# One decoder layer in fp32r passes: gate blocks as two column pairs, parked sums placed elsewhere, gelu as one ScalarE operation

## The chip, the cores and the metric

The kernel runs on one core of one Trainium2 chip. Its engines each work through their own instructions in order: TensorE (PE, matmuls), VectorE (DVE), ScalarE (ACT), GpSimd (POOL) and SyncE (SP), and the last two mostly issue DMAs. The metric is the device time of one execution in microseconds. Before the change it is 1453.33 us, the median of 3 runs (1453.3 to 1454.87).

## What is computed

One layer of a decoder trunk on 256 tokens of width 2048, all in float32: a norm, one combined projection, two attention branches (multi-head latent attention A, and banded sliding-window attention B), each passed through its output projection and multiplied by a sigmoid gate, their sum projected, and then a gated feed-forward network with a short causal convolution.

```python
  h  = RMSNorm_pre(x)
  P  = h @ W_in   # q-latent | kv-latent | rope key | SWA q, k, v | branch gates (2 x D_MODEL)
  y  = W_out( sigmoid(gA) * (A @ Wo_A) + sigmoid(gB) * (B @ Wo_B) )
  x  = x + RMSNorm_post(y)
  x  = x + RMSNorm_post2( ConvFFN( RMSNorm_pre2(x) ) )

def conv_ffn(h, w_up, conv_w, conv_b, w_down):
    a, b = jnp.split(h @ w_up, 2, axis=-1)
    ap = jnp.pad(a, ((0, 0), (CONV_WIDTH - 1, 0), (0, 0)))
    c = conv_b
    for j in range(CONV_WIDTH):
        c = c + conv_w[j] * ap[:, j:j + S]
    return (jax.nn.gelu(c, approximate=True) * b) @ w_down
```

The feed-forward width is 5632, so that the layer's weights, read once, are most of the 324 MB that it reads.

## The kernel before

**Matmuls and weights.** Every matrix product is made from three passes: both operands are split into a high part (rounded to the fp32r type) and a low part, and `mm3` (L197) adds high times high, high times low and low times high. The feed-forward up part does the same in another arrangement (`gemm_cols`, L1340 and L1344). Weights come in chunks of 512 KB on SyncE's queue into a ring of raw tiles; `convert` (L152) makes `whi` with an ACT copy (L163) and `wlo` with a DVE subtraction (L164), into a ring of converted pairs. PE uses them some chunks later, so DVE runs ahead of PE by as much as the ring holds (`RING = 4`, and two more where the flexible tiles are given to it).

**Order.** The program is written as a sequence of ticks: after each chunk of a matrix product `tick()` emits what `at(t, ...)` has booked for that tick. The instructions of each engine then stand in one fixed order, and an instruction that waits holds up all behind it on its engine.

**Seven products for eight.** `pair_gemm` (L273) computes two neighbouring column blocks of 512 together, over all 16 row blocks of the weights, in units of two row blocks. A plain unit "p" needs 24 matmuls of 512 columns (two row blocks, two token tiles, two column blocks, three passes). A unit "s" forms seven products of sums, as fast matrix multiplication does, 21 matmuls, but needs sums of token tiles (`token_sums`, here `x_sums`) and of weights: four DVE subtractions of 128x512 (`weight_sums`), and closing sums at the end. A string such as `GATE_ORDER` gives the sequence of units.

**Parked sums.** For the down products the weight sums are made ahead: `park_sums` (L237) loads two row blocks of 512 KB on POOL's queue into a staging tile, makes four subtractions in place on DVE (L252, in the order of the program: `even`, and a tick later `odd`), and stores the results to DRAM on POOL's queue (L257, L262), from where the down products load them as weights. `load` is booked 5 ticks ahead of `even`. Most units share one staging tile (`STAGE`, tag "sg"), so that a unit's load has to wait for the stores of the one before. The names in the trace are `ta_s` (the staging tile of the units for the first down products, twelve units), `ta` (the stored sums), and `tb_s`, `tc_s`, `tw_s` for others of the kind. Before the change, four of the twelve are made in the gate stage (`EARLY = 4`, with two tiles of their own), and eight in the first up part, 7.5 ticks apart (L1375).

**Gates.** Four column blocks of 512 make the B gate. `gate_b` computes one block alone, `gate_pair` two as a pair; `out_b` computes the output projection of the same columns and multiplies. Before the change the order is block 0 alone, `out_b(0)`, blocks 1 and 2 as a pair with three units "s", `out_b(1)`, block 3 alone, `out_b(2)`; `out_b(3)` stands in the latent attention. Ahead of them runs the product for the kv latent, whose result ACT reads out (L726, L727).

**First up part.** `ffn_up0` and then `ffn_up` for column blocks 1 to 5 compute the two halves `ua` and `ub` of the up projection. A block takes 16 ticks, 8 chunks for each half. The results are read out into `f` (L1361 on ACT, L1362 on DVE), and `conv_cols` (L1227) makes the convolution (`cc`, L1232 to L1234), the tanh form of gelu (`uu`, L1235 to L1238: Square, an operation of DVE, Tanh, an operation of DVE) and the product with the other half (L1239), 44 times in the run. In `ffn_up0` its input comes through transposes (`fT`).

Of the kernel before, what the change touches and what calls it, by code (L numbers as in the profile page):

```python
# [11 lines left out]
F32 = mybir.dt.float32  # L12
F32R = mybir.dt.float32r
# [6 lines left out]
P = 128  # L20
# [18 lines left out]
GELU_C = math.sqrt(2.0 / math.pi)  # L39
GELU_R = math.sqrt(0.044715)  # L40


def trunk_layer(ctx, tc, x, x_cols_in, conv_cols_in, g_mix_post, g_ffn_post, w_in, w_q, w_kv,
# [717 lines left out]
    at(now[0] + 4, lambda tr=tr: tr(1))  # L761
    acc, _ = gemm(XH, XL, w_in, 0, KT, C_KV, KVR + ROPE)
# [25 lines left out]
    def gate_b(j):  # L788
        acc, _ = gemm(XH, XL, w_in, 0, KT, C_GB + 512 * j, 512)
        tb = []  # L790
        for t in range(NT):
            g = stg(f"tb{j}_{t}")
            act.activation(g, acc[t], AF.Tanh, scale=rh[:, t:t + 1])
            tb.append(g)
        return tb

    def out_b(j, tb, ps=None):
        acc, _ = gemm(OH, OL, wo_b, 0, KT, 512 * j, 512, ps=ps)
        for t in range(NT):
            vec.scalar_tensor_tensor(tb[t], tb[t], 1.0, acc[t], op0=ALU.add, op1=ALU.mult)  # L800
            pool.dma_start(yb_d[j, t], tb[t])

    STAGE = dict(pl=base, tag="sg")
    es1.close()
    esb.close()
    esg, pg = open_pool("pg")
    xs = {}

    def x_sums(u):
        st = sb(pg, [P, 1024], f"xs{u}", F32R)  # L810
        a, m = (sb(pg, [P, 512], f"x{n}{u}", tag="x" + n, bufs=1) for n in "am")
        xs[u] = token_sums(xt[u].bitcast(F32), a, m, st[:, 0:512], st[:, 512:1024])
# [5 lines left out]
    def gate_pair(j):  # L818
        d = [stg(f"tb{j + i}_{t}") for t in range(NT) for i in range(2)]
        c = pair_gemm("g", w_in, 0, C_GB + 512 * j, GATE_ORDER, lambda k, t: (XH(k)[:, t * P:(t + 1) * P], XL(k)[:, t * P:(t + 1) * P]),  # L820
                      lambda u: xs[u], 0, d, g_place, lambda: [sb(pg, [P, 1024], f"gt{n}{cnt[0]}", tag="gt" + n, bufs=2) for n in "ab"])
# [6 lines left out]
        return [d[0], d[2]], [d[1], d[3]]  # L828

    tb = {0: gate_b(0)}  # L830
    for u in range(GATE_ORDER.count("s")):
        at(now[0] + 3 * u, lambda u=u: x_sums(u))
    out_b(0, tb[0], (pss, "s"))
    tb[1], tb[2] = gate_pair(1)
    parked_b2 = []
    parked_a = [park_a(i, pg, "gr", now[0] + 5 + 5 * i, bufs=2) for i in range(EARLY)]
    out_b(1, tb[1], (pss, "s"))
    tb[3] = gate_b(3)
    out_b(2, tb[2])
# [156 lines left out]
    out_b(3, tb[3])  # L996
# [163 lines left out]
    def x2_norm(t):  # L1160
# [66 lines left out]
    def conv_cols(k, a, b, slot):  # L1227
# [7 lines left out]
        act.activation(uu, cc, AF.Square, scale=GELU_R)  # L1235
        vec.scalar_tensor_tensor(uu, uu, 1.0, cc, op0=ALU.add, op1=ALU.mult)
        act.activation(uu, uu, AF.Tanh, scale=GELU_C)
        vec.scalar_tensor_tensor(uu, uu, 1.0, cc, op0=ALU.add, op1=ALU.mult)  # L1238
# [3 lines left out]
    def norm_row():  # L1242
# [3 lines left out]
        for t in range(NT):  # L1246
            vec.tensor_scalar(dg[:, t * P:(t + 1) * P], ident, rf[t][0][:, 0:1], None, op0=ALU.mult)
# [15 lines left out]
    def ffn_up0():  # L1263
# [88 lines left out]
    def ffn_up(c, slot0):  # L1352
# [288 lines left out]
```

## Time and profile before

| | |
|---|---|
| median of 3 runs | 1453.33 us (1453.3 to 1454.87) |
| the profiled execution, its own time | 1454.23 us |
| its span in the trace | 1452.5 us |
| granted TensorE clock, mean | 0.998 |
| matmuls in the trace | 7518 |
| busy share of DMA queue q1 (SyncE and the like), of q0 (POOL) | 59.8%, 15.0% |
| read from and written to memory | 323.6 MB, 34.7 MB |

The trace is of one execution; its own time is 1.7 us over its span (what lies around the program's instructions), and 0.9 us over the median. In the rows below, a line such as L164 is the kernel's line, then come engine, operation and tile names (result, arrow, operands, with buffer numbers left out), the shape in partitions x elements, the count, and behind a bar the busy time and the mean duration of one; the last part is the idle time ahead of these instructions and what ended it. An instruction's shown duration includes some overlap with the next on the same engine, so the distance from start to start is the better price where many follow each other.

### The profile page before, as it was taken

The page shows a single profiled execution, that of the slowest core. Times are in us where ns is not written, and L with a number is a line of the kernel's source. Part 1 is how long each engine was busy: PE and PEld are TensorE (multiplying, and loading weights), DVE is VectorE, ACT ScalarE, POOL GpSimd, SP SyncE. Part 2 cuts the span into 40 slices and gives each one's busy share as a digit, 9 for nine tenths or more (in the row PEclk, how much of TensorE's full clock was granted, in tenths as well). Part 3 has the DMA queues.
Part 4 walks back from the last instruction along what each step waited for, and adds up shares of the span by engine and source line. Part 5 has one row for each costly group of instructions (what it writes and reads, how often), then busy time and mean ns, then how long its engine had stood idle before and what let it go on. Part 6 is the DMA issues. An engine that isn't in the chain of part 4 may idle for free.

```text
span 1452.5 us, 21438 instructions
## 1 busy us (share of the span) xinstructions
PE 1442.0 (99%) x7518; PEld 1233.7 (85%) x7518; DVE 1160.4 (80%) x2056; ACT 864.7 (60%) x1422; POOL 118.2 (8%) x222
## 2 busy tenths in 40 slices
PE   9999999999999999999999999999999999999997
PEld 7888888888898888888888888888888888888886
DVE  7788896766878775888789899876777797987798
ACT  7588864544555655546566565655646565555673
POOL 2022110010000001100000111000000101000000
PEclk9999999999999999999999999999999999999999
DMA  8655376699875759965666898866878888789965
GB/s 309 209 171 163 103 261 188 219 327 294 244 220 178 230 164 319 348 232 183 219 205 208 272 331 288 292 206 210 310 276 262 312 276 292 246 265 309 340 219 203
DMA packets 164684, 359.69 MB, mean 248 GB/s; under 512 B 20816, under 2 KB 31952, under 8 KB 164576
## 3 DMA queue, kind: packets, MB, share of 16 engines
q1 hardware_dynamic: 143152, 282.49, 59.8%
q0 software_dynamic: 21280, 75.56, 15.0%
q8 instruction: 59, 0.97, 0.3%
q14 instruction: 49, 0.40, 0.1%
q10 hardware_dynamic: 144, 0.26, 0.1%
HBM read 323.62 MB, written 34.65 MB: 247 GB/s over the span
## 4 chain that ended last, share of the span: by engine, by line
PE 91%; DVE 4%; ACT 2%; DMA 2%; issue 1%; SPq 0%; DVEq 0%; ACTq 0%
PE ub L1340 10%; PE ua L1340 9%; PE accg L200 9%; PE accg L198 9%; PE accg L199 9%; PE ub L1344 5%; PE ua L1344 5%; PE cd L199 2%; PE cd L198 2%; PE cd L200 2%; DVE wlo L164 2%; DMA raw<-in_ffn_w_up_dram 1%; PE cdc L199 1%; PE cdc L198 1%; PE cdc L200 1%
## 5 line engine op out<-in xcount | busy, mean ns | idle before, releaser
L163 ACT CAST whi<-raw 128x1024 fp32r<-128x1024 f32 (+2 forms) x497 | 504.0, 1023 | 373.9 <-PE accg L200 109.1
L164 DVE TENSOR_TENSOR wlo<-raw,whi 128x1024 fp32r<-128x1024 f32 (+2 forms) x497 | 585.0, 1188 | 172.0 <-ACT whi L163 165.6
L198 PE MATMUL accg<-whi,ahl 128*128 128x512 f32 (+1 forms) x416 | 162.5, 391 | 0.0
L200 PE MATMUL accg<-whi,ahl 128*128 128x512 f32 (+1 forms) x416 | 160.7, 386 | 0.0
L199 PE MATMUL accg<-wlo,ahl 128*128 128x512 f32 (+1 forms) x416 | 159.8, 384 | 0.0
L1340 PE MATMUL ub<-ahl,whi 128*128 128x512 f32 x640 | 154.7, 391 | 0.2 <-DVE uu L1239 0.2
L1340 PE MATMUL ua<-ahl,whi 128*128 128x512 f32 x640 | 154.6, 391 | 0.0
L1340 PEld LDWEIGHTS ub<-ahl,whi 128*128 128x128 f32 x640 | 117.5, 188 | 23.1 <-ACT cc L1232 0.5
L1340 PEld LDWEIGHTS ua<-ahl,whi 128*128 128x128 f32 x640 | 117.6, 188 | 22.7
L198 PE MATMUL accg<-whi,bhl 128*128 128x512 f32 x256 | 100.8, 394 | 0.0
L200 PE MATMUL accg<-whi,bhl 128*128 128x512 f32 x256 | 100.0, 391 | 0.0
L199 PE MATMUL accg<-wlo,bhl 128*128 128x512 f32 x256 | 99.9, 390 | 0.0
L200 PEld LDWEIGHTS accg<-whi,ahl 128*128 128x128 f32 x416 | 78.1, 188 | 15.2
L199 PEld LDWEIGHTS accg<-wlo,ahl 128*128 128x128 f32 x416 | 78.3, 188 | 13.0
L198 PEld LDWEIGHTS accg<-whi,ahl 128*128 128x128 f32 x416 | 78.2, 188 | 12.9
L1344 PEld LDWEIGHTS ub<-ahl,wlo 128*128 128x128 f32 x640 | 82.2, 191 | 3.3
L1344 PEld LDWEIGHTS ua<-ahl,wlo 128*128 128x128 f32 x640 | 82.2, 191 | 3.1
L1344 PE MATMUL ua<-ahl,wlo 128*128 128x256 f32 x640 | 83.7, 283 | 0.0
L1344 PE MATMUL ub<-ahl,wlo 128*128 128x256 f32 x640 | 83.3, 283 | 0.0
L200 PEld LDWEIGHTS accg<-whi,bhl 128*128 128x128 f32 x256 | 48.1, 188 | 10.1
L199 PEld LDWEIGHTS accg<-wlo,bhl 128*128 128x128 f32 x256 | 48.1, 188 | 9.6
L198 PEld LDWEIGHTS accg<-whi,bhl 128*128 128x128 f32 x256 | 48.1, 188 | 9.6
(659 smaller groups left out, 2679.7 us busy)
## 6 DMA issues: line engine op xcount, KB each, us to landing
raw<-in_ffn_w_up_dram SPq DMA_DIRECT2D x142, 512.0 KB, 4.9
raw<-in_w_in_dram SPq DMA_DIRECT2D x105, 512.0 KB, 4.6
raw<-in_ffn_w_down_dram SPq DMA_DIRECT2D x66, 512.0 KB, 5.6
xraw<-in_ffn_w_up_dram SPq DMA_DIRECT2D x34, 512.0 KB, 5.2
raw<-in_w_o_swa_dram SPq DMA_DIRECT2D x32, 512.0 KB, 5.3
raw<-in_w_o_mla_dram SPq DMA_DIRECT2D x26, 512.0 KB, 6.9
raw<-in_w_out_dram SPq DMA_DIRECT2D x26, 512.0 KB, 4.6
ta_s<-in_ffn_w_down_dram POOLq DMA_DIRECT2D x24, 512.0 KB, 5.9
```

The source lines that it names most:

```text
L163: act.copy(hi[:, a:b], raw[:, a:b])
L164: vec.tensor_tensor(lo[:, a:b], raw[:, a:b], hi[:, a:b].bitcast(F32), op=ALU.subtract)
L198: pe.matmul(o, ah, bh, start=start, stop=False)
L199: pe.matmul(o, ah, bl, start=False, stop=False)
L200: pe.matmul(o, al, bh, start=False, stop=stop)
L1340: pe.matmul(acc[i], hi[:, c], hn[p][:, j * 512:(j + 1) * 512], start=p + j == 0, stop=stop)
L1344: pe.matmul(acc[i][:, 0:256], lo[:, c], hn[p][:, j * 512:j * 512 + 256], start=False, stop=False)
```

## The change

Three things are changed.

The four gate blocks become two pairs, (0, 1) and (2, 3), each with three units "s". The sums of the token tiles are made earlier, in the product for the kv latent, and the pool that they lie in is opened there. `out_b` takes its gate tiles through a function, since the pair's tiles are made when its closing sums are.

Of the twelve parked units for the first down products, none is made in the gates any more. Two are made in the latent attention (`EARLY = 2`), through the common staging tile, behind the `tw` and `tc0` units, which stand 6 ticks apart in place of 7. The other ten stand in the first up part, 6 ticks apart in place of 7.5, starting at the fifth tick in place of the eighth.

Gelu is one ACT operation in place of Square, Tanh and two DVE operations. The factor 0.5 that the tanh form needed goes out of the read-out of `f`, whose operations become a plain copy and a plain addition. The size of a filler tile (`LINE_Z`) becomes 64 in place of 48.

```diff
--- before.py
+++ after.py
@@ -36,8 +36,6 @@
 C_GA = 3392
 C_GB = 5440
-GELU_C = math.sqrt(2.0 / math.pi)
-GELU_R = math.sqrt(0.044715)
 
 
 def trunk_layer(ctx, tc, x, x_cols_in, conv_cols_in, g_mix_post, g_ffn_post, w_in, w_q, w_kv,
@@ -759,6 +757,24 @@
     nrm()
     at(now[0] + 3, lambda tr=tr: tr(0))
     at(now[0] + 4, lambda tr=tr: tr(1))
+    STAGE = dict(pl=base, tag="sg")
+    xs = {}
+
+    def x_sums(u):
+        st = sb(pg, [P, 1024], f"xs{u}", F32R)
+        a, m = (sb(pg, [P, 512], f"x{n}{u}", tag="x" + n, bufs=1) for n in "am")
+        xs[u] = token_sums(xt[u].bitcast(F32), a, m, st[:, 0:512], st[:, 512:1024])
+
+    def to_gates():
+        nonlocal esg, pg
+        es1.close()
+        esb.close()
+        esg, pg = open_pool("pg")
+
+    esg = pg = None
+    at(now[0] + 4, to_gates)
+    for u in range(GATE_ORDER[0].count("s")):
+        at(now[0] + (5, 7, 11)[u], lambda u=u: x_sums(u))
     acc, _ = gemm(XH, XL, w_in, 0, KT, C_KV, KVR + ROPE)
     krd = []
     for t in range(NT):
@@ -785,58 +801,40 @@
     yb_d = dram.tile([4, NT, P, 512], F32, name="yb_d")
     x2_d = dram.tile([NT, P, D], F32, name="x2_d")
 
-    def gate_b(j):
...
-        return tb
-
-    def out_b(j, tb, ps=None):
+    def out_b(j, tb_of, ps=None):
         acc, _ = gemm(OH, OL, wo_b, 0, KT, 512 * j, 512, ps=ps)
+        tb = tb_of()
         for t in range(NT):
             vec.scalar_tensor_tensor(tb[t], tb[t], 1.0, acc[t], op0=ALU.add, op1=ALU.mult)
             pool.dma_start(yb_d[j, t], tb[t])
 
-    STAGE = dict(pl=base, tag="sg")
-    es1.close()
-    esb.close()
-    esg, pg = open_pool("pg")
...
     def g_place():
         both = sb(pg, [P, D], f"gr{cnt[0]}", tag="gr", bufs=2)
         return both[:, 0:1024], both[:, 1024:2048]
 
-    def gate_pair(j):
-        d = [stg(f"tb{j + i}_{t}") for t in range(NT) for i in range(2)]
-        c = pair_gemm("g", w_in, 0, C_GB + 512 * j, GATE_ORDER, lambda k, t: (XH(k)[:, t * P:(t + 1) * P], XL(k)[:, t * P:(t + 1) * P]),
-                      lambda u: xs[u], 0, d, g_place, lambda: [sb(pg, [P, 1024], f"gt{n}{cnt[0]}", tag="gt" + n, bufs=2) for n in "ab"])
+    def gate_pair(j, order):
+        d = []
+
+        def gate_tiles():
+            d[:] = [stg(f"tb{j + i}_{t}") for t in range(NT) for i in range(2)]
+            return d
+
+        c = pair_gemm(f"g{j}", w_in, 0, C_GB + 512 * j, order, lambda k, t: (XH(k)[:, t * P:(t + 1) * P], XL(k)[:, t * P:(t + 1) * P]),
+                      lambda u: xs[u], 0, gate_tiles, g_place, lambda: [sb(pg, [P, 1024], f"gt{n}{cnt[0]}", tag="gt" + n, bufs=2) for n in "ab"])
         def finish_gate(i):
             vec.tensor_tensor(d[i], d[i], c[i], op=ALU.add)
             act.activation(d[i], d[i], AF.Tanh, scale=rh[:, i // 2:i // 2 + 1])
 
         for n_, i in enumerate((0, 2, 1, 3)):
             at(now[0] + n_, lambda i=i: finish_gate(i))
-        return [d[0], d[2]], [d[1], d[3]]
-
-    tb = {0: gate_b(0)}
-    for u in range(GATE_ORDER.count("s")):
-        at(now[0] + 3 * u, lambda u=u: x_sums(u))
-    out_b(0, tb[0], (pss, "s"))
-    tb[1], tb[2] = gate_pair(1)
+        return lambda i: (d[i], d[2 + i])
+
+    tb = gate_pair(0, GATE_ORDER[0])
     parked_b2 = []
-    parked_a = [park_a(i, pg, "gr", now[0] + 5 + 5 * i, bufs=2) for i in range(EARLY)]
-    out_b(1, tb[1], (pss, "s"))
-    tb[3] = gate_b(3)
-    out_b(2, tb[2])
+    for j in range(2):
+        out_b(j, lambda j=j: tb(j), None if j else (pss, "s"))
+    tb = gate_pair(2, GATE_ORDER[1])
+    out_b(2, lambda: tb(0), (pss, "s"))
     esg.close()
 
 
@@ -985,15 +983,16 @@
         at(t0 + 6, lambda: pt(0), lambda: pt(1))
         at(t0 + 7, lambda: pv(0), lambda: pv(1))
 
-    parked_w = [park_sums(f"tw{i}_", wo_a, 2 * i, 0, t0=now[0] + 7 + 7 * i, **STAGE) for i in range(NA_)]
-    parked_b2.append(park_sums("tc0_", w_down, 24, 1024, t0=now[0] + 7 + 7 * NA_, **STAGE))
+    parked_w = [park_sums(f"tw{i}_", wo_a, 2 * i, 0, t0=now[0] + 7 + 6 * i, **STAGE) for i in range(NA_)]
+    parked_b2.append(park_sums("tc0_", w_down, 24, 1024, t0=now[0] + 7 + 6 * NA_, **STAGE))
+    parked_a = [park_a(i, t0=now[0] + 13 + 6 * (NA_ + i), **STAGE) for i in range(EARLY)]
     b = now[0] + 2
     for u in range(8):
         if u % 4 == 0:
             q_rope8(u // 4, b + 4 * u)
         mla_unit(u, b + 4 * u)
 
-    out_b(3, tb[3])
+    out_b(3, lambda: tb(1))
     at_ = [slot("b", p) for p in range(8)]
     ath[:], atl[:] = highs(at_), lows(at_)
     for j in range(4):
@@ -1164,9 +1163,7 @@
         vec.tensor_reduce(v, ssh[t], axis=AX.X, op=ALU.add)
         vec.tensor_scalar(v, v, 1.0 / D, EPS, op0=ALU.mult, op1=ALU.add)
         r = rsqrt(v, 1, f"rf{t}", p3)
-        r2 = sb(p3, [P, 1], f"rfh{t}")
-        vec.tensor_scalar(r2, r, 0.5, None, op0=ALU.mult)
-        rf[t] = (r, r2)
+        rf[t] = r
 
     w_done = [0]
 
@@ -1232,10 +1229,7 @@
         act.activation(cc, a, AF.Identity, scale=w2, bias=cb_)
         vec.scalar_tensor_tensor(cc[:, 1:256], a[:, 0:255], w1, cc[:, 1:256], op0=ALU.mult, op1=ALU.add)
         vec.scalar_tensor_tensor(cc[:, 2:256], a[:, 0:254], w0, cc[:, 2:256], op0=ALU.mult, op1=ALU.add)
-        act.activation(uu, cc, AF.Square, scale=GELU_R)
-        vec.scalar_tensor_tensor(uu, uu, 1.0, cc, op0=ALU.add, op1=ALU.mult)
-        act.activation(uu, uu, AF.Tanh, scale=GELU_C)
-        vec.scalar_tensor_tensor(uu, uu, 1.0, cc, op0=ALU.add, op1=ALU.mult)
+        act.activation(uu, cc, AF.Gelu_apprx_tanh)
         vec.tensor_tensor(uu, uu, b, op=ALU.mult)
         split_to(GH(slot), GL(slot), uu)
 
@@ -1244,7 +1238,7 @@
         row = sb(base, [P, NT, 4, 64], "row", tag="rtab").rearrange("p a b c -> p (a b c)")
         r, dg = row[:, 0:256], row[:, 256:512]
         for t in range(NT):
-            vec.tensor_scalar(dg[:, t * P:(t + 1) * P], ident, rf[t][0][:, 0:1], None, op0=ALU.mult)
+            vec.tensor_scalar(dg[:, t * P:(t + 1) * P], ident, rf[t][:, 0:1], None, op0=ALU.mult)
         pr = pst.tile([P, 512], F32, name="rrow", tag="t")
         pe.matmul(pr[:, 0:256], ones_p, dg, start=True, stop=True)
         act.copy(r, pr[:, 0:256])
@@ -1268,7 +1262,7 @@
             f = sb(p6, [P, 1024], f"f{q}_0", tag="f" + "ab"[q], bufs=2)
             for t in range(NT):
                 a = f[:, t * 512:(t + 1) * 512]
-                act.activation(a, acc[t], AF.Copy, scale=rf[t][q][:, 0:1])
+                act.activation(a, acc[t], AF.Copy, scale=rf[t][:, 0:1])
                 sa[t][q] = a
 
         def cols(i):
@@ -1357,9 +1351,8 @@
             f = sb(p6, [P, 1024], f"f{q}_{c}", tag="f" + "ab"[q], bufs=2)
             for i in range(4):
                 a = f[:, i * 256:i * 256 + 256]
-                sc = (1.0, 0.5)[q]
-                act.activation(a, acc[i][:, 256:512], AF.Copy, scale=sc)
-                vec.scalar_tensor_tensor(a, acc[i][:, 0:256], sc, a, op0=ALU.mult, op1=ALU.add)
+                act.copy(a, acc[i][:, 256:512])
+                vec.tensor_tensor(a, acc[i][:, 0:256], a, op=ALU.add)
                 sa[q].append(a)
 
         acc = [pacc.tile([P, 512], F32, name=f"ua{c}_{i}", tag="acc") for i in range(4)]
@@ -1373,7 +1366,7 @@
 
     es7 = ffn_up0()
     for i in range(sum(NA) - EARLY):
-        parked_a.append(park_a(i + EARLY, t0=now[0] + 8 + 15 * i // 2, **STAGE))
+        parked_a.append(park_a(i + EARLY, t0=now[0] + 5 + 6 * i, **STAGE))
     for c in range(1, 6):
         if c == 2:
             for i in range(8):
@@ -1561,13 +1554,13 @@
 RING = 4
 A_ORDER = "ppspspsp"
 NA_ = A_ORDER.count("s")
-GATE_ORDER = "psppspsp"
+GATE_ORDER = ("pppspssp", "psppspsp")
 B_ORDER = "psspsspssp"
 B2_ORDER = "ppsspssppp"
 NB2 = B2_ORDER.count("s")
 W_ORDER = "ppspspsp"
 PAIR_ORDER = ("pppspsspsssp", "ppspspsspssp")
-EARLY = 4
+EARLY = 2
 NA = [o.count("s") for o in PAIR_ORDER]
 NB_ = B_ORDER.count("s")
 XCUT = [0, 1, 2, 3, 4, 6, 8, 10, 12, 14, 16]
@@ -1578,7 +1571,7 @@
 LINE_A = 80
 LINE_B = 80
 LINE_W = 64
-LINE_Z = 48
+LINE_Z = 64
 RAW = 3
 STG = 4
```

The lines of the changed kernel differ by a few: L162 is the conversion (before: L164), L250 the parked subtraction (L252), L196 to L198 the three passes (L198 to L200).

On PE, at the start of the gates, this stood before (`accg_0` and `accg_1` are two accumulators, first the last rows of the kv product with 320 columns, then the gate block with 512; `whi`, `wlo` the weights):

```order
L198 MATMUL accg_1_2269<-whi_2511,ahl_170 128x320
L199 MATMUL accg_1_2269<-wlo_2512,ahl_170 128x320
L200 MATMUL accg_1_2269<-whi_2511,ahl_170 128x320
L198 MATMUL accg_0_2572<-whi_2576,ahl_163 128x512
L199 MATMUL accg_0_2572<-wlo_2577,ahl_163 128x512
L200 MATMUL accg_0_2572<-whi_2576,ahl_163 128x512
L198 MATMUL accg_1_2573<-whi_2576,ahl_163 128x512
```

and this stands there now:

```order
L198 MATMUL accg_1_2269<-whi_2526,ahl_170 128x320
L196 MATMUL cg_0_2592<-whi_2598,ahl_166 128x512
...
L196 MATMUL cg_1_2593<-whi_2598,ahl_166 128x512
...
L196 MATMUL cg_0_2592<-whi_2616,ahl_166 128x512
L197 MATMUL cg_0_2592<-wlo_2617,ahl_166 128x512
L198 MATMUL cg_0_2592<-whi_2616,ahl_166 128x512
L196 MATMUL cg_2_2594<-whi_2598,ahl_166 128x512
```

The pair `cg` has four accumulators in place of two, and the third is first written by the tenth of its matmuls.

On DVE, in the first up part, these rows of before follow the last subtraction of one parked unit (the first row); behind them stand 17 more rows, four conversions among them, until the next unit's first subtraction:

```order
L252 TENSOR_TENSOR ta_s<-ta_s 128x512
L1236 SCALAR_TENSOR_TENSOR uu_8618<-uu_8618,cc_8617 128x256
L1234 SCALAR_TENSOR_TENSOR cc_8678<-f_1_8236,cvT,cc_8678 128x254
L164 TENSOR_TENSOR wlo_8514<-raw_8511,whi_8513 128x1024
L1238 SCALAR_TENSOR_TENSOR uu_8618<-uu_8618,cc_8617 128x256
L380 TENSOR_TENSOR sm_9458<-sa_9457 128x128
L164 TENSOR_TENSOR wlo_8540<-raw_8537,whi_8539 128x1024
L381 TENSOR_TENSOR sm_9458<-sa_9457 128x128
L382 TENSOR_TENSOR sm_9458<-sm_9458,sa_9457 128x128
L383 TENSOR_TENSOR sm_9458<-sa_9457,sm_9458 128x128
L377 TENSOR_TENSOR sa_9549<-bhl_7761 128x512
L1362 SCALAR_TENSOR_TENSOR f_1_8437<-ub_0_8245,f_1_8437 128x256
```

In the changed kernel, a little later in the same part, the whole stretch from one unit's last subtractions to the first of the next is this:

```order
L250 TENSOR_TENSOR ta_s<-ta_s 128x512 x3
L162 TENSOR_TENSOR wlo_8763<-xraw_8738,whi_8762 128x1024
L162 TENSOR_TENSOR wlo_8785<-raw_8782,whi_8784 128x1024
L1355 TENSOR_TENSOR f_2_8697<-ua_0_8461,f_2_8697 128x256
L1355 TENSOR_TENSOR f_2_8697<-ua_1_8462,f_2_8697 128x256
L1355 TENSOR_TENSOR f_2_8697<-ua_2_8463,f_2_8697 128x256
L1355 TENSOR_TENSOR f_2_8697<-ua_3_8464,f_2_8697 128x256
L162 TENSOR_TENSOR wlo_8806<-xraw_8738,whi_8805 128x1024
L1230 SCALAR_TENSOR_TENSOR cc_8956<-f_2_8697,cvT,cc_8956 128x255
L162 TENSOR_TENSOR wlo_8828<-raw_8825,whi_8827 128x1024
L250 TENSOR_TENSOR ta_s<-ta_s 128x512
```

There are nine rows between the units where there were 28. The gelu rows (`uu`, L1236 and L1238) are gone from it, and the units follow each other sooner.

On ACT, at the first gelu of the run, this stood before:

```order
L1232 ACTIVATE cc_8028<-fT_8023,cvT 128x256
L1235 ACTIVATE uu_8029<-cc_8028 128x256
L163 CAST whi_8216<-raw_8214 128x1024
L1237 ACTIVATE uu_8029<-uu_8029 128x256
L1232 ACTIVATE cc_8072<-fT_8067,cvT 128x256
```

and this stands there now:

```order
L1229 ACTIVATE cc_8052<-fT_8047,cvT 128x256
L161 CAST whi_8234<-raw_8232 128x1024
L1232 ACT_TABLE_LOAD
L1232 ACTIVATE uu_8053<-cc_8052 128x256
L1229 ACTIVATE cc_8093<-fT_8088,cvT 128x256
```

One operation stands in place of two, and a table load ahead of the first of them, the only one that is added.

More of the change, by code (lines that the diff above doesn't have):

```diff
@@ L786, in trunk_layer @@
     x2_d = dram.tile([NT, P, D], F32, name="x2_d")
-    def gate_b(j):
[L789 to L794, printed above, removed]
-        return tb
-    def out_b(j, tb, ps=None):
+    def out_b(j, tb_of, ps=None):
         acc, _ = gemm(OH, OL, wo_b, 0, KT, 512 * j, 512, ps=ps)
+        tb = tb_of()
         for t in range(NT):
@@ L801, in out_b @@
             pool.dma_start(yb_d[j, t], tb[t])
-    STAGE = dict(pl=base, tag="sg")
-    es1.close()
-    esb.close()
-    esg, pg = open_pool("pg")
[L807 to L812, printed above, removed]
     def g_place():
```

## The prediction

> **What bounds the kernel now.** I read the page first, then the windows of the stages that the change touches, then the waits of TensorE.
>
> ```profile
> span 1452.5 us, 21438 instructions
> PE 1442.0 (99%) x7518; PEld 1233.7 (85%) x7518; DVE 1160.4 (80%) x2056; ACT 864.7 (60%) x1422; POOL 118.2 (8%) x222
> ```
>
> TensorE (PE) is busy for 1442.0 of 1452.5 us; VectorE (DVE) has 20% of its time free, ScalarE (ACT) 40%. So time is won only by taking matmuls away, and work taken off DVE or ACT is worth nothing by itself. It is lost where something makes PE late. The windows tell how much room each stage leaves; the columns are busy time and count for PE, PEld, DVE, ACT and POOL, then granted clock, DMA share and GB/s.
>
> ```profile
> 198.00:240.00 42.00, 42.00 (x190) 34.72 (x189) 33.74 (x65) 21.13 (x29) 2.39 (x5) 1.00 0.77 250
> 385.00:560.00 175.00, 175.00 (x1058) 155.04 (x1057) 128.33 (x266) 98.92 (x182) 17.24 (x32) 1.00 0.70 219
> 802.00:1000.00 198.00, 197.98 (x1135) 174.91 (x1136) 165.16 (x281) 114.59 (x187) 14.94 (x28) 1.00 0.82 277
> ```
>
> These are the gates, the latent attention and the first up part. PE has no gap in any of them, DVE is 80, 73 and 83% busy, and in the last one DMA is the fullest of the three, at 277 GB/s. What PE waits for, in the whole run, is this list (engine and line, what it waited for, us, times, longest):
>
> ```profile
> PE warm L76 <- DVE ramp L67: 1.1, 1, 1.1
> PE acckv L199 <- DVE wlo L164: 0.4, 1, 0.4
> PE ub L1340 <- DVE uu L1239: 0.2, 1, 0.2
> ```
>
> There is next to nothing to win from waits.
>
> **Part 1, the gate blocks: −2.0 us.** Counted in the order of both kernels, PE loses 9 matmuls of 512 columns (7555 to 7546) and nothing else: each of three more seven-product units issues 21 where a plain unit issues 24. Their price is PE's cadence in a bare gemm, from the chain of work (start, us, what):
>
> ```profile
> 702.54 0.23 PE accg L198
> ...
> 704.81 0.23 PE accg L199
> ```
>
> Ten steps in 2.27 us are 0.227 us each, so 9 × 0.227 = 2.0 us. A first gate pair now follows the latent-kv gemm directly, and it takes four accumulator banks where one block took two. The matmuls into the third bank come tenth (the first 9 fill 2.0 us from 196.27, where the first gate matmul starts in the trace of before), that is at 198.3, while ScalarE still reads the kv result out:
>
> ```profile
> 196.27 0.39 PE L198 MATMUL accg<-whi,ahl 128*128 128x512 f32 x1
> 198.36 0.41 ACT L727 ACTIVATE accg<-ck 128x256 f32<-128x256 f32 x1
> 198.66 0.22 ACT L727 ACTIVATION_READ_ACCUMULATOR accg<-ck 128x1 f32 x1
> ```
>
> That ends at 198.9, so I add +0.6 us; the bounds are 0, if the pair's banks are others, and 1.2, if that copy slips by as much again. DVE's additions (6 conversions at 1.14, 12 weight sums and 8 closing sums at 0.6: 18.8 us, by the rows of part 2) are spread over two pairs of 183 × 0.227 = 41.5 us. One pair needs some 20.5 conversions, 12 weight sums and 8 closing sums, 35.4 us, and is hidden under its 41.5; if that cover were gone the excess would be PE's. The x sums move up into the kv gemm, which costs PE nothing as long as DVE keeps its 20%.
>
> **Part 2, the parked sums: the term that decides.** A parked unit goes through one staging tile: two 512 KB loads on POOL's queue, four DVE subtractions in place, two stores on the same queue, and only when those have landed the next loads. POOL's timeline shows the chain (start, us, what, in brackets the idle time before and its releaser):
>
> ```profile
> 838.07 0.54 POOL L262 DMA_DIRECT2D ta<-ta_s  x1 [3.47 <-DVE ta_s L252]
> 843.56 1.06 POOL L245 DMA_DIRECT2D ta_s<-in_ffn_w_down_dram  x2 [4.96 <-DMA ta<-ta_s]
> ...
> 894.51 0.55 POOL L262 DMA_DIRECT2D ta<-ta_s  x1 [2.20 <-DVE ta_s L252]
> 902.90 1.06 POOL L245 DMA_DIRECT2D ta_s<-in_ffn_w_down_dram  x2 [7.85 <-DMA ta<-ta_s]
> ```
>
> From the second store's issue to the next load's issue it takes 5.5 us here and 8.4 there; the eight units of this stage give 6.4 in the mean. Then the load, in the query of DMA transfers (KB each, median us to landing) and where DVE already waits for it:
>
> ```profile
> ta_s<-in_ffn_w_down_dram POOLq DMA_DIRECT2D x14, 512.0 KB, 6.1
> 849.70 0.69 DVE L252 TENSOR_TENSOR ta_s<-ta_s 128x512 f32<-128x512 f32 x1 [0.64 <-DMA ta_s<-in_ffn_w_down_dram]
> 851.74 0.69 DVE L252 TENSOR_TENSOR ta_s<-ta_s 128x512 f32<-128x512 f32 x1 [1.01 <-DMA ta_s<-in_ffn_w_down_dram]
> ```
>
> The first half landed 849.70 − 843.56 = 6.1 us after the issue, the second 8.2 us after it. The 6.1 of the first row is a median over both halves; the first half is the quicker one, and I take 5.4 for it, an estimate. So from a unit's last subtraction to the next unit's first stand 6.4 + 5.4 = **11.8 us**. DVE runs in order: a subtraction that comes to the head of its queue sooner waits, and behind it wait the weight conversions that PE needs next. Even at today's distance the row above shows waits of 0.6 and 1.0 us.
>
> Today the units are 7.5 ticks apart, after the change 6 ticks, ten units in place of eight. One tick of this stage is 2.78 us:
>
> ```profile
> 818.71 1.98 PE L1340 MATMUL ua<-ahl,whi 128*128 128x512 f32 x8
> ...
> 840.98 1.98 PE L1340 MATMUL ub<-ahl,whi 128*128 128x512 f32 x8
> ```
>
> (22.27 us for a block of eight). So 20.9 us shrink to 16.7. But what counts is what DVE has to do between two units. Start-to-start prices come from DVE's timeline and the chain:
>
> ```profile
> 787.76 0.68 DVE L252 TENSOR_TENSOR ta_s<-ta_s 128x512 f32<-128x512 f32 x1
> 788.37 0.41 DVE L1239 TENSOR_TENSOR uu<-uu,fT 128x256 f32<-128x256 f32 x1
> ...
> 794.64 1.14 DVE wlo L164
> 795.78 0.33 DVE uu L1239
> 796.11 0.39 DVE cc L1233
> ```
>
> A subtraction is 0.61, a conversion 1.14, a 256-column operation 0.33, a convolution step 0.39. With them the order of before has 8 to 15 us of DVE work from a unit's last subtraction to the next unit's first, mostly 13 to 15: longer than 11.8, no wait. In the changed order the nine distances are 7.3, 5.0, 5.9, 6.3, 5.7, 8.5, 10.2, 7.2 and 4.9 us, 61 in sum; the 6.3 is the pair of units shown with the change (four conversions, four f sums, one convolution step: 4.56 + 1.32 + 0.39). Nine chains take 9 × 11.8 = 106 us, so DVE waits some 45 us, and about 0.5 us a unit more for second halves, as in the row at 851.74: **50 us**. What can absorb them is DVE's free time and its lead. Between the first unit's last subtraction and the tenth's first stand 48 conversions, which PE takes 48 × 2.78 = 133.7 us to use; DVE's work there is 61 + 45 (the units themselves, with what stands inside them) = 106 us; 27.7 are free. Left are 22.3. The lead is read from conversions and the matmuls that use them:
>
> ```profile
> 817.86 1.23 DVE L164 TENSOR_TENSOR wlo<-raw,whi 128x1024 fp32r<-128x1024 f32 x1 [1.02 <-ACT whi L163]
> 826.09 2.08 PE L1344 MATMUL ua<-ahl,wlo 128*128 128x256 f32 x16
> ...
> 844.21 1.22 DVE L164 TENSOR_TENSOR wlo<-raw,whi 128x1024 fp32r<-128x1024 f32 x1
> 853.93 2.08 PE L1344 MATMUL ub<-ahl,wlo 128*128 128x256 f32 x16
> ```
>
> By tile names the first is used by the second half of its x16 row, at 827.0, 8.0 us after it ends; the other at 854.85, 9.4 us after. I take 8, bounds 5 and 11. So PE is late by 22.3 − 8 = **+14 us**. The bounds of the sum: nothing, if the chain takes 10.2 us or less (9 × 1.6 = 14); +23 us, if it takes 12.8.
>
> The two units that go into the latent attention add 8 subtractions, 4.9 us, to 175 us in which DVE has 47 free; its 40 ticks are 4.4 us each, so 6 ticks are 26 us, over twice the chain: no wait. On POOL's queue the y loads stand behind them, and POOL is 10% busy there. The four early units leave the gates, which gives DVE 9.8 us there and PE nothing.
>
> **Part 3, gelu on ScalarE: 0 to −1 us.** The groups that go (busy us, mean ns):
>
> ```profile
> L1236 DVE SCALAR_TENSOR_TENSOR uu<-uu,cc 128x256 f32<-128x256 f32 x44 | 18.0, 418 | 0.6 <-ACT uu L1235 0.5
> L1238 DVE SCALAR_TENSOR_TENSOR uu<-uu,cc 128x256 f32<-128x256 f32 x44 | 18.0, 417 | 0.0
> L1235 ACT ACTIVATE uu<-cc 128x256 f32<-128x256 f32 x44 | 17.6, 413 | 10.5 <-DVE cc L1234 9.1 <-DVE bhl L417 0.6
> ```
>
> 88 × 0.33 = 29 us of DVE and 44 × 0.41 = 18 us of ACT, both beside PE; the relief of DVE is already in the 61 and 45 above. PE gains only where it waits for this chain, at the start of the first up part:
>
> ```profile
> 801.55 0.28 PE L1344 MATMUL ub<-ahl,wlo 128*128 128x256 f32 x1
> 802.02 0.70 PE L1340 MATMUL ub<-ahl,whi 128*128 128x512 f32 x2 [0.19 <-DVE uu L1239]
> ```
>
> A matmul of 256 columns takes 0.12 from start to start, so PE loses 802.02 − 801.55 − 0.12 = 0.35 us here; I credit 0.4 with the transposes before, bounds 0 and 1. The scaled f copies become plain ones of the same shape: nothing. One table load comes onto ACT; the tail has one now:
>
> ```profile
> 1399.71 1.28 ACT L1515 ACT_TABLE_LOAD   x1
> 1401.01 0.20 ACT L1515 ACTIVATE first<-ssz 128x1 f32<-128x1 f32 x1
> ```
>
> So 1.3 us on an engine that is 42% free there. The Trainium skill, page "ScalarE: Activation LUTs", section "What ACT_TABLE_LOAD costs", gives 1283 ns for the load and some 1380 ns of drain, 2.66 us a switch; the load agrees with the trace, the drain is not seen behind it. By that page ACT would stand 1.4 us longer, under a lead of 8 us, and the sum would be the same.
>
> **The sum.** The profiled execution took 1454.2 us, 1.7 more than its span and 0.9 more than the median of 1453.3. 1454.2 − 2.0 + 0.6 − 0.4 + 14 = 1466.4, and 0.9 less as a median: **1465.5 us**.
>
> **Rivals.**
> *The lead holds* (other side). If the landings are quicker than in before, 10.2 us for the chain, nothing reaches PE: 1453.3 − 1.8 = 1451.5. For it: the store-to-load time was 5.5 at 838, and SyncE's queue, whose weight loads share the DMA engines, already waits much for DVE (us, times, longest), so they pause when DVE does:
>
> ```profile
> SPq L142 <- DVE wlo L164: 100.7, 42, 5.9
> ```
>
> Against it: it was 8.4 at 894, and loads and stores both come denser.
>
> *No wait and the gaps closed*: the lead holds, the banks are free, and the relief of DVE closes 1 us of small gaps like that at 802: 1453.3 − 2.0 − 1.1 = 1450.2. For it: the shorter gelu chain; against it: PE's 197.98 of 198 us, there is hardly a gap to close, and the rows of L727.
> *A longer chain*: ten units, each 1 MB in and 1 MB out, stand where eight did (10 × 16.7 = 8 × 20.9 = 167 us), some 4.2 MB more or 25 GB/s on 277; at 12.8 us the loss is 23 us and the time 1474.5.
> The Trainium skill, page "SBUF — State Buffer", section "SBUF: two separate sides", warns that DMAs issued from POOL's queue can starve while VectorE runs certain copies; that would act as this rival does, and no row here separates it from plain traffic.
> *The gates cost more than they save*: DVE at 35.4 of 41.5 us has 6 us a pair; if the units come late by 3 us in each pair, 1453.3 + 4 = 1457. Against it: conversions run ahead here too.
>
> **Chances.** Forecast 0.50, longer chain 0.10, the lead holds 0.24, gaps closed 0.12, gates 0.04. A measurement can tell 0.2%, 2.9 us, from no change. Faster by more: the gaps' 0.12 and 0.04 of the lead's; within: 0.20 of the lead's and 0.03 of small losses; slower: the rest, 0.61. The range of 8 in 10 runs from 1451 to 1475.
>
> **What would show it.** Right: waits of DVE for the landing of ta_s of some 40 to 50 us in all, PE waiting for wlo in the first up part by 14 us, the stage from the first f transposes to the down products longer by as much, PE's matmuls shorter by 2.0 us. Wrong: units 17 us apart with PE unbroken would mean that I read the lead too small or the chain too long; PE gaps in the gate pairs would mean part 1; a gap of PE behind the table load, part 3.

## The result and the profile after

The changed kernel takes 1480.16 us (median of 6 runs, 1477.44 to 1485.16), the kernel before, on the same chip, 1454.43 us. The ratio is 1.0177 (95% interval 1.0154 to 1.0199): it is slower by 1.8%, about 26 us. The forecast was slower, 1465.5 us with 1475 as the upper end; so the direction was right and the size was about half of what came. Ratios here and below compare executions in the chip's usual state; single ones of three variants below (2408.50, 2920.71 and 5300.70 us) were in a slow state and stand in no ratio, though their variants' medians count them.

The page of the changed kernel, its span and the busy times:

```profile
span 1478.7 us, 21322 instructions
PE 1450.4 (98%) x7509; PEld 1237.0 (84%) x7509; DVE 1148.0 (78%) x1992; ACT 854.8 (58%) x1386; POOL 121.5 (8%) x228
```

PE has 9 matmuls fewer and yet is busy for 8.4 us more (1442.0 before). A busy engine that does less work in more time runs more slowly; that is the first thing to see here. What PE waits for, in the whole run:

```profile
PE ua L1338 <- DVE wlo L162: 11.1, 6, 4.1
PE ub L1334 <- ACT whi L161: 3.6, 1, 3.6
PE ub L1338 <- DVE wlo L162: 2.4, 3, 1.5
PE warm L74 <- DVE ramp L65: 1.1, 1, 1.1
PE cw L196 <- DVE lta L1063: 0.7, 1, 0.7
PE qg L197 <- DVE wlo L162: 0.4, 1, 0.4
PE qg L196 <- ACT whi L161: 0.2, 1, 0.2
```

The first three rows, 17.1 us, are new, and all are in the first up part: PE waits for converted weights. What VectorE waits for there, from the groups of the page:

```profile
L250 DVE TENSOR_TENSOR ta_s<-ta_s 128x512 f32<-128x512 f32 x48 | 33.0, 687 | 50.0 <-DMA ta_s<-in_ffn_w_down_dram 49.8
```

Before it was 1.9 us with 1.7 for the DMA; now it is 50.0, of which 49.8 end with the landing of a parked unit's load. The chain of work in this stage shows one full cycle of a unit (start, us, what):

```profile
867.63 6.23 DMA ta<-ta_s
873.86 0.02 issue
873.88 0.02 POOLq L243
873.90 0.52 issue
874.42 0.53 POOL ta_s L243
874.95 7.42 DMA ta_s<-in_ffn_w_down_dram
```

Store 6.2 us, issue, load 7.4 us: for 14 us the chain of the run isn't on PE at all, and stands on the one staging tile. From the second store's issue to the next unit's first subtraction the nine cycles take 9.1 to 14.5 us, 11.9 in the mean; the eight later ones alone 12.3. And the windows of the stage (columns as above), first the five in which PE waits most, then the whole stage, from 773 to just behind the start of the down products:

```profile
857.00:867.00 10.00, 6.36 (x27) 5.02 (x27) 6.10 (x10) 3.21 (x5) 0.54 (x1) 0.83 0.57 206
879.00:897.00 18.00, 14.39 (x65) 12.13 (x65) 15.12 (x29) 8.05 (x12) 2.15 (x4) 0.81 0.67 230
921.00:932.00 11.00, 6.91 (x32) 5.97 (x32) 7.80 (x10) 2.25 (x5) 1.08 (x2) 0.84 0.56 188
942.00:950.00 8.00, 5.73 (x31) 4.53 (x31) 5.84 (x10) 4.16 (x6) 0.54 (x1) 1.00 0.49 168
961.00:973.00 12.00, 10.00 (x48) 8.36 (x48) 9.95 (x18) 5.95 (x10) 1.08 (x2) 0.86 0.59 199
773.00:1033.00 260.00, 242.81 (x1335) 211.44 (x1334) 184.02 (x296) 129.15 (x204) 21.42 (x40) 0.97 0.76 256
```

The same stage in the kernel before:

```profile
773.00:1007.00 234.00, 233.81 (x1338) 206.03 (x1337) 195.89 (x337) 138.19 (x227) 17.07 (x32) 1.00 0.80 265
```

The matmuls are the same but for the windows' edges, so the 26.0 us more split in two: PE stands idle for 17.0 us more (260 − 242.81 = 17.2 against 0.2), and it takes 242.81 − 233.81 = 9.0 us longer for the same work, at a granted clock of 0.97 in place of 1.00. Outside this stage nothing is left: the first matmul of the down products (`cd`) starts at 1023.0 in place of 996.8, 26.2 us later, and the spans differ by 1478.7 − 1452.5 = 26.2 us.

The slower clock is a state of its own, not an average. The clock of the changed kernel reads 1.00 until 862.5, then 0.50 until 865.9, then 1.00 again; and 0.50 from 886.4 to 893.2, from 927.4 to 930.8 and from 968.3 to 971.8. In steps of 1 us the first fall and the first rise show as 0.76 and 0.53, since each lies inside a step. The clock falls where PE has just stood still:

```profile
862.00:863.00 1.00, 0.05 (x1) 0.05 (x1) 1.00 (x3) 1.00 (x2) 0.03 (x1) 0.76 0.00 0
865.00:866.00 1.00, 1.00 (x4) 0.81 (x3) 1.00 (x2) 0.24 (x1) 0.00 (x0) 0.53 0.35 139
...
862.95 3.48 PE L1334 MATMUL ub<-ahl,whi 128*128 128x512 f32 x8 [3.64 <-ACT whi L161]
886.34 2.03 PE L1338 MATMUL ua<-ahl,wlo 128*128 128x256 f32 x8 [3.22 <-DVE wlo L162]
890.63 5.03 PE L1334 MATMUL ua<-ahl,whi 128*128 128x512 f32 x16
```

Eight matmuls of 512 columns take 3.48 us here, and 1.98 in the rows of before. The four stretches of half clock are 17.1 us together, and PE works in 15.7 of them; half of that, 7.9 us, is what the clock costs. It is most of the 9.0 us. The other 1.1 us are not separated further; part of them goes with the waits themselves, since two rows of eight that a wait parts take 1.22 us each where a row of sixteen takes 2.08.

### The profile page after: what moved, and what is told of

It reads as the page before. It is cut to its first block, busy times and chain, and to the rows that moved or that the text cites. A ratio compares the mean times of both kernels' runs of the same rounds, so it can differ in the third digit from the quotient of the medians.

```text
span 1478.7 us, 21322 instructions
## 1 busy us (share of the span) xinstructions
PE 1450.4 (98%) x7509; PEld 1237.0 (84%) x7509; DVE 1148.0 (78%) x1992; ACT 854.8 (58%) x1386; POOL 121.5 (8%) x228
## 5 line engine op out<-in xcount | busy, mean ns | idle before, releaser
L162 DVE TENSOR_TENSOR wlo<-raw,whi 128x1024 fp32r<-128x1024 f32 (+2 forms) x491 | 577.3, 1188 | 167.0 <-ACT whi L161 160.9
L161 ACT CAST whi<-raw 128x1024 fp32r<-128x1024 f32 (+2 forms) x491 | 497.2, 1023 | 360.7 <-PE accg L198 98.7
L196 PE MATMUL accg<-whi,ahl 128*128 128x512 f32 (+1 forms) x352 | 137.5, 391 | 0.0
L198 PE MATMUL accg<-whi,ahl 128*128 128x512 f32 (+1 forms) x352 | 135.7, 385 | 0.0
L197 PE MATMUL accg<-wlo,ahl 128*128 128x512 f32 (+1 forms) x352 | 134.9, 383 | 0.0
L196 PE MATMUL accg<-whi,bhl 128*128 128x512 f32 x256 | 100.7, 393 | 0.0
L198 PE MATMUL accg<-whi,bhl 128*128 128x512 f32 x256 | 99.9, 390 | 0.0
L1338 PE MATMUL ua<-ahl,wlo 128*128 128x256 f32 x640 | 87.9, 290 | 11.1 <-DVE wlo L162 11.1
L198 PEld LDWEIGHTS accg<-whi,ahl 128*128 128x128 f32 x352 | 66.1, 188 | 12.8
L196 PEld LDWEIGHTS accg<-whi,ahl 128*128 128x128 f32 x352 | 66.2, 188 | 10.7
L197 PEld LDWEIGHTS accg<-wlo,ahl 128*128 128x128 f32 x352 | 66.2, 188 | 10.5
L250 DVE TENSOR_TENSOR ta_s<-ta_s 128x512 f32<-128x512 f32 x48 | 33.0, 687 | 50.0 <-DMA ta_s<-in_ffn_w_down_dram 49.8
L198 PEld LDWEIGHTS accg<-whi,bhl 128*128 128x128 f32 x256 | 48.1, 188 | 10.1
L196 PEld LDWEIGHTS accg<-whi,bhl 128*128 128x128 f32 x256 | 48.1, 188 | 9.7
```

The costliest lines, as they stand in the source:

```text
L161: act.copy(hi[:, a:b], raw[:, a:b])
L162: vec.tensor_tensor(lo[:, a:b], raw[:, a:b], hi[:, a:b].bitcast(F32), op=ALU.subtract)
L196: pe.matmul(o, ah, bh, start=start, stop=False)
L197: pe.matmul(o, ah, bl, start=False, stop=False)
L198: pe.matmul(o, al, bh, start=False, stop=stop)
L250: tc.keep_in_program_order(vec.tensor_tensor(o, x, y, op=ALU.subtract))
```

## The experiments

Theory: the parked units of the first up part stand too close for their one staging tile; VectorE waits at the head of its queue, PE runs out of converted weights, and each idle stretch that is long enough is followed by a half clock. Rivals: gelu or the gate pairs cost the time; the DMA engines are too full; the half clock has another cause than idle time.

### The spacing put back

```diff
-        parked_a.append(park_a(i + EARLY, t0=now[0] + 5 + 6 * i, **STAGE))
+        parked_a.append(park_a(i + EARLY, t0=now[0] + 5 + 15 * i // 2, **STAGE))
```

> The changed kernel with one number put back: the ten parked units of the first up part 7.5 ticks apart in place of 6, all else as changed. Chain theory (one staging tile, store and load of 11.8 us between two units, units too close): DVE's waits for the landing of ta_s fall from 49.8 us to under 6, TensorE's 17 us of waits in the stage to under 1, its clock stays at 1.00 in every window, and the time is 1453 to 1454.5 us, within 0.2% of before. Rival, the loss comes from the gelu operation or from the gate pairs: the time stays above 1470.

It took 1454.21 us against 1453.35, ratio 1.0004 (0.9995 to 1.0012): the whole loss is gone, with gelu and the gate pairs in place. VectorE's waits were 7.7 us, a little more than expected, and nothing of the stage is in PE's list any more:

```profile
PE warm L74 <- DVE ramp L65: 1.1, 1, 1.1
PE cw L196 <- DVE lta L1063: 0.5, 1, 0.5
PE qg L197 <- DVE wlo L162: 0.4, 1, 0.4
PE acckv L509 <- ACT whi L161: 0.2, 1, 0.2
PE qg L196 <- ACT whi L161: 0.2, 1, 0.2
```

### The parked units alone

The kernel before, with the parked units where the change has them:

```diff
-    parked_a = [park_a(i, pg, "gr", now[0] + 5 + 5 * i, bufs=2) for i in range(EARLY)]
...
+    parked_a = [park_a(i, t0=now[0] + 13 + 6 * (NA_ + i), **STAGE) for i in range(EARLY)]
...
-        parked_a.append(park_a(i + EARLY, t0=now[0] + 8 + 15 * i // 2, **STAGE))
+        parked_a.append(park_a(i + EARLY, t0=now[0] + 5 + 6 * i, **STAGE))
...
-EARLY = 4
+EARLY = 2
```

> The kernel before with the parked units alone moved (two in the latent attention, ten in the first up part 6 ticks apart), gates and gelu as before. Chain theory: DVE waits 30 to 50 us for ta_s, TensorE's clock falls below 0.98 in the stage, and the time is 1470 to 1482 us. Rival, the spacing hurts only together with the shorter gelu or the gate pairs: below 1458.

1480.42 us, ratio 1.0172 (1.0153 to 1.0191): the changed kernel's loss, with none of its other parts. VectorE waited 43.7 us for ta_s, PE 18.4 us for converted weights, and the granted clock of the run was 0.992, as in the changed kernel. So the shorter gelu is not what makes the units too close. The two runs together show that the placing of the parked units is enough for the loss, and that of this placing the 6 ticks between the ten units are needed for it.

### A second staging tile for two units

```diff
-        parked_a.append(park_a(i + EARLY, t0=now[0] + 5 + 6 * i, **STAGE))
+        parked_a.append(park_a(i + EARLY, t0=now[0] + 5 + 6 * i, **(dict(pl=p3, tag="x2_0") if i in (4, 6) else STAGE)))
```

> The changed kernel with a second staging tile (one that is free from the middle of column block 2 to block 4) for two of the ten parked units, the fifth and the seventh, the same 6 ticks apart and the same bytes. Chain theory: the waits at the fifth to eighth unit (7.0 + 0.5, 7.5 + 0.5, 1.5 + 1.5, 4.6 + 1.7, 25 us in all) fall to under 8, the TensorE gaps of 3.6, 3.2 and 4.1 us near 861, 885 and 926 go, and the time falls by 10 to 18 us, to 1462 to 1470. Rival, the DMA engines are simply too full in this stage: the waits stay above 18 us and the time above 1474.

1457.47 us, ratio 1.0026 (1.0014 to 1.0038): 23 us came back, more than I had expected, from the same spacing and the same bytes. VectorE waited 19.6 us in all. Of the fifth to eighth unit's 25 us there were 1.8 + 2.1 us at the fifth, none at the next two, and 0.8 + 0.3 at the eighth. The window of 850 to 930 shows that full DMA engines were not the limit: with the second tile they carry more.

```profile
850.00:930.00 80.00, 79.40 (x455) 69.63 (x454) 68.12 (x116) 43.02 (x68) 9.62 (x18) 1.00 0.91 323
```

In the changed kernel the same window has 249 GB/s, and PE is busy for 68.66 of 80 us:

```profile
850.00:930.00 80.00, 68.66 (x363) 59.54 (x363) 54.48 (x92) 35.84 (x57) 8.03 (x15) 0.92 0.74 249
```

That is the mark of a chain: everything is less busy at once. More came back than the waits of these four units. One reason stands in the rows: the clock stays at 1.00. The other I infer: VectorE still waits 6.5 us at the ninth unit, but PE waits there for 0.5 us at the longest, in place of 1.4, so VectorE seems to come to it with its lead restored.

### 7 and 6.5 ticks

The same line with `7 * i`, and with `13 * i // 2`.

> The changed kernel with the ten parked units of the first up part 7 ticks apart in place of 6, all else as changed. Chain theory: 7 ticks are 19.5 us, the cycle of the changed kernel's units is 16 to 21 us (units' starts from 808.4 to 962.4, eight cycles, 19.3 us in the mean with the losses in it), so most waits go but not all: DVE waits 10 to 25 us for ta_s in place of 49.8, VectorE's lead takes them, and the time is 1453.5 to 1457 us. Rival, any spacing under 7.5 ticks loses in proportion (a third of the way back): about 1462 us.

> The changed kernel with the ten parked units 6.5 ticks apart in place of 6. 6 ticks gave 49.8 us of DVE waits and 26 us of loss, 7 ticks gave 30.7 us of waits and no loss. Lead theory: only what goes beyond VectorE's free time and its lead is lost, so about 40 us of waits here leave 4 to 12 us of loss with the clock's share: 1458 to 1466 us. Rival, loss in proportion to the waits: no such step, and since 30.7 us cost nothing it would be nothing here too, below 1456.

7 ticks: 1455.02 us, ratio 1.0008 (0.9999 to 1.0017), VectorE's waits 30.7 us, PE's waits in the stage 1.5. 6.5 ticks: 1461.04 us, ratio 1.0048 (1.0034 to 1.0062), VectorE's waits 30.8 us, PE's waits 4.7. With 6 ticks it was 49.8 and 17.1. So the loss grows faster than the spacing shrinks, about 1 us at 7 ticks, 7 at 6.5 and 26 at 6, and 30 us of VectorE's waits can cost next to nothing; that fits a lead which is used up first. But my 40 us of waits for 6.5 ticks were wrong: the same 30 us give 1.5 us of PE's waits in one order and 4.7 in the other, and the sum of VectorE's waits alone doesn't tell the loss. The lead itself was not read in these two runs.

The run with 6.5 ticks also separates the two losses. Its waits are short, and the clock stays whole:

```profile
920.61 1.22 PE L1338 MATMUL ua<-ahl,wlo 128*128 128x256 f32 x8 [1.81 <-DVE wlo L162]
...
790.00:1010.00 220.00, 215.34 (x1221) 188.36 (x1220) 169.47 (x275) 116.73 (x187) 20.82 (x39) 1.00 0.83 282
```

PE's longest wait is 1.8 us, the clock reads 1.00, and the matmuls behind it run at full speed.

### Idle time without any parked unit

The kernel before, with one useless reduction on VectorE in each of five column blocks, as long as the numbers say:

```diff
+    def idle(k):
+        dz = sb(base, [P, NT, 4, 64], "dz", tag="rtab").rearrange("p a b c -> p (a b c)")
+        vec.memset(dz[:, 0:256], 0.0)
+        tc.keep_in_program_order(vec.tensor_reduce(dz[:, 256:256 + k], dz[:, 0:256].unsqueeze(1).to_broadcast([P, k, 256]), axis=AX.X, op=ALU.add))
+
     for c in range(1, 6):
+        at(now[0] + 12, lambda c=c: idle((36, 40, 44, 50, 60)[c - 1]))
```

> The kernel before with one useless reduction on VectorE in each of the column blocks 1 to 5 of the first up part (36, 40, 44, 50 and 60 times 256 elements, 9 to 16 us each by some 1.04 ns an element, an estimate from the 128x512 subtraction's 0.61 us taken at its slope), so that TensorE stands idle for some 0 to 8 us each time, with no parked unit involved. Clock theory: gaps under about 3 us leave the granted clock at 1.00, longer ones are followed by 0.50 for 3.4 or 6.8 us, and each such gap costs 1.7 to 3.4 us beyond its own length. Rival, the half clock in the changed kernel comes from the DMA traffic or the parked units: the clock stays at 1.00 here whatever the gap.

A single run, 1499.96 us, 46 more than the kernel before. The reductions took 9.8 to 16.1 us. PE's rows behind the gaps:

```profile
788.44 1.22 PE L1344 MATMUL ua<-ahl,wlo 128*128 128x256 f32 x8 [1.82 <-DVE wlo L164]
804.83 2.07 PE L1344 MATMUL ub<-ahl,wlo 128*128 128x256 f32 x8 [2.15 <-DVE wlo L164]
857.60 3.81 PE L1344 MATMUL ub<-ahl,wlo 128*128 128x256 f32 x16 [7.49 <-DVE wlo L164]
898.94 3.75 PE L1340 MATMUL ub<-ahl,whi 128*128 128x512 f32 x8 [5.38 <-DVE f L1362]
977.25 2.08 PE L1344 MATMUL ub<-ahl,wlo 128*128 128x256 f32 x8 [5.56 <-DVE wlo L164]
1031.40 2.08 PE L1344 MATMUL ub<-ahl,wlo 128*128 128x256 f32 x8 [8.91 <-DVE wlo L164]
```

Behind the wait of 1.8 us eight matmuls of 256 columns take 1.22 us; behind 2.2 us and all longer ones they take nearly twice as long. The windows around two of the gaps give the clock (last but two of the columns):

```profile
802.00:805.00 3.00, 0.85 (x7) 0.65 (x6) 2.64 (x6) 2.94 (x6) 0.00 (x0) 0.94 0.41 165
805.00:808.00 3.00, 3.00 (x12) 2.71 (x13) 3.00 (x4) 0.00 (x0) 0.54 (x1) 0.50 0.59 173
808.00:812.00 4.00, 4.00 (x23) 3.49 (x22) 3.39 (x7) 1.47 (x2) 0.00 (x0) 0.99 0.85 267
...
978.00:983.00 5.00, 5.00 (x18) 4.18 (x17) 5.00 (x9) 1.04 (x1) 0.54 (x1) 0.58 0.72 197
983.00:990.00 7.00, 7.00 (x48) 6.41 (x47) 6.30 (x14) 5.44 (x11) 1.06 (x2) 1.00 0.95 336
```

So the half clock follows idle time of PE and needs neither parked units nor their DMAs. It read 0.50 from 804.7 to 808.1 behind the shortest gap that caused it, and from 975.3 to 982.2 around a longer one; half of the time in which PE worked at it, 1.6 and 2.5 us, was lost. My bound of about 3 us was too high: 2.2 us was enough once, and a single gap of 1.8 us was not, here and with 6.5 ticks.

The length of the gap is not the whole of it. In the clock records of these traces the stretches of half clock are whole multiples of 3.41 us long, and within a run they begin and end at times that differ by whole multiples of it, as if on one grid. Ahead of each of the fourteen falls that a wait brought (in the changed kernel, the parked units alone, this run and the gate pairs below) PE had stood idle for 1.65 us or more of the grid's last step; in the steps behind which the clock stayed whole it was 1.8 us at most. So it counts where in the grid a gap lies: the gap of 1.8 us above falls on two steps, about 1.0 us in the first and 0.8 in the second.

The Trainium skill, page "TensorE: Matmul & The Clock Gate", section "What's actually happening", has this as two states, half rate after an idle window of about 3.4 us and full rate after a busy one of the same length, and the section "Why this matters for your kernels" asks for no gap over about 3 us. The halves and their length agree with these windows; a gap as short as 2.2 us is below what it names.

### Gelu, and the gate pairs

Gelu alone, on the kernel before (the change's lines of `conv_cols`, of the read-out of `f` and of the 0.5, and the larger filler tile):

> The kernel before with the gelu part of the change alone. Chain theory: nothing waits on it, 1453.5 to 1454.5 us against 1454.4, DVE about 29 us less busy. Rival, the table load or the new order on ScalarE disturbs the up part: above 1457.

1452.83 us, ratio 0.9996 (0.9987 to 1.0005): no difference that can be told, with 27 us less work on VectorE (1133.4 us busy).

The gate pairs alone, with four parked units behind the first pair, in the two tiles of the gate stage that the kernel before gave them. The edit is shown against the changed kernel, whose other parts (gelu, distances, `EARLY`, filler tile) are put back as before:

```diff
+    parked_a = [park_a(i, pg, "gr", now[0] + 5 + 5 * i, bufs=2) for i in range(EARLY)]
     for j in range(2):
```

> The kernel before with the gate pairs alone; gelu and the placing of the parked units as before (four in the gate stage, behind the first pair). By the 9 matmuls it is 2.0 us faster; by the waits that the changed kernel's trace shows in the first pair (0.2, 0.59 and 0.33 us) 0.9 us of that stay: 1452.5 to 1454, within 0.2% of before. Rival, VectorE can't carry the first pair with the parked units beside it: above 1456.

1466.79 us, ratio 1.0081 (1.0067 to 1.0094). This was not a run of the gate pairs alone, as I had meant, since the second pair now needs the two tiles that the parked units hold:

```profile
295.25 0.69 DVE L230 TENSOR_TENSOR gta<-gr 128x512 f32<-128x512 f32 x1 [10.98 <-DMA gr<-in_w_in_dram]
...
299.59 0.79 PE L198 MATMUL cg<-whi,ahl 128*128 128x512 f32 x1 [10.61 <-ACT whi L163]
```

The load of the pair's weights is issued at 290.95, after 11.05 us behind a parked unit's store; VectorE waits 11 us for these weights, and PE 10.6 us behind it. The clock reads 0.50 from 292.0 to 305.7 around this wait, far from the up part, and 0.994 in the mean of the run. It shows why the early units can't stay in the gate stage with two pairs.

The changed kernel with 7.5 ticks and with the gelu of before:

> The changed kernel with the ten parked units 7.5 ticks apart and with the gelu of before (Square, Tanh and two VectorE operations): the gate pairs without gelu and without the short spacing, and without the collision that the run of the gate pairs alone had, since no parked unit uses the gate stage's tiles. If the gate pairs bring their 2.0 us less the 1.1 us of waits in the first pair: 1452.5 to 1454.5 us, DVE waits under 10 us for ta_s. Rival, the gate pairs need the relief of the gelu: above 1457.

1453.87 us, ratio 1.0005 (0.9996 to 1.0015). The gate pairs don't need the relief of gelu, and their 2.0 us don't show in the time. In the trace of the changed kernel PE loses 1.1 us in the first pair (0.20, 0.59 and 0.33), where VectorE is busy for 41.85 of 42 us:

```profile
198.00:240.00 42.00, 41.44 (x182) 33.30 (x183) 41.85 (x79) 24.56 (x32) 5.14 (x10) 1.00 0.65 227
```

No version that I ran is told apart from the kernel before on the fast side; gelu alone comes nearest.

## Why the prediction was right or wrong, by its steps

**What bounds the kernel** held: PE, and a loss comes where something makes it late.

**The parked sums.** The mechanism is the one that was predicted, and the two runs on the placing show it. The chain of 11.8 us was 11.9 in the mean of nine, though its halves were not as priced: store and issue took 5.8 us for 6.4, the first half of the load 6.2 for 5.4. VectorE's 50 us of waits were 49.8, and here too two errors cancel: the waits for first halves were 42.5 us for 45, those for second halves 7.3 for 5. That both sums came out so closely is partly luck. The lateness of PE, 22.3 − 8 = 14 us, measured 17.0. Since VectorE's waits were as forecast, the 3 us lie in the other two terms, the 27.7 us of free time or the lead of 8, which the runs don't separate.

**The step that failed** is the one behind it: "So PE is late by 22.3 − 8 = +14 us", taken as the whole loss. It left out that PE, once idle, comes back at half clock. Four of the idle stretches were followed by half clock, and the same matmuls took 9.0 us longer, 7.9 of them by the clock. 17.0 + 9.0 in place of 14 in the forecast's sum, 1466.4, gives 1478.4; the profiled execution took 1480.5. Most of the rest is the 1.8 us that the gates and gelu were to bring on balance and that did not show. The upper end of the range was made with idle time only as well (+23 us for a longer chain), so it missed too. The kernel before could not show this: its longest wait of PE is 1.1 us, and its clock reads 1.00 until 1447 us, 5 us from the end.

**The gates**, −2.0 and +0.6. The 9 matmuls are gone (7518 to 7509 in the traces), but no run shows their 2.0 us in the time; the waits were +1.1 by the gaps of the trace, in place of 0.6. I had put VectorE's room in the pair at 6 us and named the third bank as the only wait; the bank cost 0.2, and the late conversions, in a stretch where VectorE has no room at all, 0.9. The 0.7 us ahead of `cw` belong to no part of the change: 0.8 us stand there also in the run with idle time, whose program is that of before up to that place, and none in the run with the gate pairs and the old gelu.

**Gelu**, 0 to −1 us: 0.5 us faster by the medians, within the uncertainty. The table load took 1.28 us and the next operation began behind it at once, off the path, as the sum had it:

```profile
780.76 1.28 ACT L1232 ACT_TABLE_LOAD   x1
782.06 0.42 ACT L1232 ACTIVATE uu<-cc 128x256 f32<-128x256 f32 x1
```

**The latent attention** took the two units without a wait: none of VectorE's waits for ta_s lies before 800 us.

**The rivals.** The longer chain, 12.8 us, did not come: the chain was 11.9, and the time passed that rival's 1474.5 by the half clock. The lead did not hold. That the DMA engines are too full was wrong, by the second tile's 323 GB/s.

## What to carry to other kernels

Before work that goes through one buffer is moved closer together, compare the buffer's whole round trip (store, issue, load) with the work of the waiting engine between two uses, in that engine's own order; a distance in loop steps doesn't tell it. When TensorE's idle time is priced, add the half clock: in these runs every gap over 2.1 us cost another 1.5 to 3.2 us, and waits of up to 1.8 us, alone, cost nothing of the kind, so the same idle time is cheaper in short pieces. And an edit that only relieves an engine beside the bound can be worth nothing until something uses the relief: gelu alone took 27 us of work off VectorE and changed no time.

## What was not expected of the hardware

The half clock set in behind a gap of PE of 2.2 us, but not behind one of 1.8 us. It came in pieces of 3.4 us, one to four of them, all on one grid of 3.4 us. Around the gap of 7.5 us it read 0.50 from 852.5 to 862.7, of which the last 5 us were work. In the changed kernel two shorter waits close together were enough as well:

```profile
966.95 1.22 PE L1338 MATMUL ub<-ahl,wlo 128*128 128x256 f32 x8 [1.48 <-DVE wlo L162]
968.69 2.08 PE L1338 MATMUL ub<-ahl,wlo 128*128 128x256 f32 x8 [0.52 <-DVE wlo L162]
```

The second eight matmuls run at half speed, the first eight don't. The clock fell at 968.3, inside the second wait; the 3.4 us that ended there hold the first wait and the beginning of the second, 1.65 us of idle time in all. A gap of 1.8 us inside one such step, with 6.5 ticks, was not followed by half clock, so these runs give no sharp limit.
